# Weight sums of the MLP made once and kept in DRAM, in a trunk kernel whose order comes from the scheduler's detailed simulation

## The chip, the cores and the metric

The kernel runs on one core of one Trainium2 chip. The metric is the device time in microseconds of one execution; the median of three runs is compared, and the profile is of one more execution.

## The reference

One decoder layer over 2048 tokens of width 1024, in float32, with 256 memory tokens beside them:

```python
h = rmsnorm(x, mix_norm_g);  q, k, v, g, u = split(h @ w_in)
x = x + concat([silu(g) * head_rmsnorm(retention(rope(q), rope(k), v)), pool_mixer(u)]) @ w_out
x = x + cross_attn(rmsnorm(x, xa_norm_g), mem_n, xa_wq, xa_wkv, xa_wo)
a = rmsnorm(x, ffn_norm_g) @ w_up                  # 1024 -> 2 * 2816
c = conv_w[0] * a[t-2] + conv_w[1] * a[t-1] + conv_w[2] * a[t] + conv_b
x = x + (silu(c[gate half]) * c[value half]) @ w_down    # 2816 -> 1024
out = rmsnorm(x, final_norm_g)
```

## The kernel before

Tokens go in two batches of 1024 (`NB` = 2, `T` = 1024), each in two halves of 512 (`SUB`). Activations lie with channels on the 128 partitions. A product in full precision is made of three passes in float32r (`passes`, lines 227 to 229): each operand is split into a rounded high part, written by ScalarE, and the rest, written by VectorE or GpSimd.

**First stages, for each batch.** `unit` (line 271) makes one 128-wide output tile: `load_tile` (line 286) has SyncE's queue fetch 512 KB of weights into a raw buffer in tile `R`, `pairs` splits it into tile `Q` (lines 219 and 202), and 48 matmuls follow. Retention, pooling, the output projection, cross-attention and its projection are made of such units. Between them small matmuls of retention run, which `behind` hands out in steps: line 716 makes the scores of a head from its rotated q and k, and the last step of a rotation is an add on GpSimd (`tt(pool, d, d, w)` in `rope_evac`, tiles `Z<-Z,T`). During the first batch the stages fold weights as well (`folded_weights`, loads on line 403). Raw buffers: `R` holds five of 1024 columns.

**The MLP** is run by `run`. Both products use a scheme of seven products in place of eight: the weights of two output tiles and two halves of the inner dimension are blocks a11, a12, a21, a22, and the right side has two halves of channels and of tokens. A `Member` is one such pair of output tiles: `Up` (22 a batch) and `Down` (4 a batch in each of three rounds of inner tiles, with 3, 4 and 4 tiles a half). It has seven items, and each item needs one combination of the weight blocks and one of the right side:

- *Weights.* `fetch` loads four blocks of 256 KB (192 KB in the rounds of 3), and `add` makes a11 - a21, then a21 + a22, then that less a11, then a12 less that: four adds on GpSimd, tiles `R<-R`, line 202. `high` and `low` (lines 989 and 202) split the item's combination into a pair buffer. The tuple `how` says for each of the seven items who makes the low part: `""` VectorE, `"copy"` VectorE from a PSUM copy that ScalarE makes first (line 894), `"pool"` GpSimd.
- *Right side.* `combining` makes the tile in `G` for item i: it loads one or two pieces (`T<-Hd` or `T<-Gd`), subtracts on GpSimd if there are two (`T<-T`), and splits them (line 928 and 202). The tiles of the next round replace those of the last one as its last members are done with them, so they are made in the time of a few items at every change of round.
- *PE* runs an item as 12 matmuls (9 in the rounds of 3) into a PSUM bank. `evac` adds the banks up on VectorE; for `Up` the convolution, SiLU and the gate follow (lines 1064 to 1084), and the result goes to DRAM (`Gd`).

`run` writes the program in the order of the items with fetches, sums and splits some items ahead. At the end of each batch's last round the sums of squares are reduced by tiny matmuls (line 296) for the final norm, followed by two matmuls a half that spread the factors (line 1218).

What is written is not yet the order on the engines: the Tile framework's scheduler simulates the program, and puts on each engine next what is ready in that simulation. Each engine, and SyncE's queue of DMAs, then goes through its list strictly in order.

Of the kernel before, what the change touches and what calls it, by code (L numbers as in the profile page):

```python
# [29 lines left out]
TW = 576  # L30
EDGE = 16

_PI = 314159265358979323846264338327950288419716939937510582097494459
# [84 lines left out]
def trunk(ctx, tc, xT, memT, pos, w_qkgu, w_v, wkv, wqT, wo, wout_r, wout_p, poolT, w_up, w_dn, vecs, consts, outT):  # L118
# [82 lines left out]
    def tt(eng, out, a, b, op):  # L201
        return eng.tensor_tensor(out=out, in0=a, in1=b, op=op)  # L202
# [59 lines left out]

    behind = [iter(())]

# [4 lines left out]
    def unit(raw, rhs, evac, order=range(4)):  # L269


        hs = pairs(raw)
        ps = [mmps() for _ in range(NS)]
        for h in range(2):
            for s in range(NS):
                for j, kk in enumerate(order):
                    k = 4 * h + kk
                    w = [hs[h][:, i, kk * P : (kk + 1) * P] for i in range(2)]
                    passes(ps[s], w, rhs(k, s), h + j == 0, h == 1 and j == 3)
                next(behind[0], None)  # L280
                if h == 1:
                    evac(s, ps[s])
# [517 lines left out]
    def attention(sums, beside):  # L800
# [37 lines left out]
        for i in range(2 * KT):  # L838
# [20 lines left out]
            if late is not None:  # L859
                turn(*late)  # L860
            late = prob[hp], t, e
            next(more_m if i < KT - 2 else beside, None)

# [3 lines left out]
        return prob, end()  # L867

# [76 lines left out]
    class Member:  # L945


        def __init__(self, loads, halves):
            self.loads, self.n = loads, halves

            self.sign, self.how = 1, ("", "copy", "copy", "", "copy", "copy", "")
            self.raw = {}

        def fetch(self):

            g, h = ((0, 0), (1, 0), (1, 1), (0, 1))[len(self.raw)]
            w = self.n * P
            r = raws.take()
            sp.dma_start(r.f[:, :w], self.loads[g][:, h * w : (h + 1) * w])
            self.raw[g, h] = r  # L960

        def add(self, i):

            while len(self.raw) < (1, 2, 3, 3, 3, 4, 4)[i]:
                fetches.pop(0).fetch()
            w = self.n * P
            q = {k: r.f[:, :w] for k, r in self.raw.items()}
            a11, a12, a21, a22 = (q.get(k) for k in ((0, 0), (0, 1), (1, 0), (1, 1)))
            self.t = None
            if i == 1:  # L970
                self.t = H.take()
                x = self.t.f[:, :w]
                tt(pool, x, *((a11, a21) if self.sign > 0 else (a21, a11)), ALU.subtract)
            elif i == 2:

                tt(pool, a21, a21, a22, ALU.add)
                tt(pool, a11, a21, a11, ALU.subtract)
                x = a11
            elif i == 5:
                tt(pool, a11, a12, a11, ALU.subtract)  # L980
                x = a11
            else:
                x = {0: a11, 3: a22, 4: a21, 6: a12}[i]
            return x, self.t

        def high(self, i, x, pr):
            w = self.n * P
            p2 = pr.r.rearrange("p (i n) -> p i n", i=2)
            act.activation(p2[:, 0, :w], x, AF.Copy)  # L989
            return p2[:, 0, :w], p2[:, 1, :w]  # L990

        def low(self, i, x, t, hi, lo):
            low(x, hi, lo, self.how[i])
            if t is not None:
                t.free()
            if i >= 3:
                self.raw[{3: (1, 1), 4: (1, 0), 5: (0, 0), 6: (0, 1)}[i]].free()

# [3 lines left out]
    class Up(Member):  # L1002


        def __init__(self, b, f):
            super().__init__([w_up[f + g * NF].rearrange("p k n -> p (k n)") for g in range(2)], 4)
            self.b, self.f, self.how = b, f, ("", "copy", "copy", "", "copy", "copy", "pool")
            self.c = {}
# [81 lines left out]
    class Down(Member):  # L1090
# [3 lines left out]
        def __init__(self, b, j, at, k0, halves):  # L1094
            super().__init__([w_dn[2 * j + g][:, k0 : k0 + 2 * halves].rearrange("p k c -> p (k c)") for g in range(2)], halves)
            self.b, self.j, self.at, self.sign = b, j, at, -1

# [163 lines left out]
    def rounds():  # L1261
        out = []
        for b in range(NB):
            ups = [Up(b, f) for f in range(NF)]
            groups = [ups[:2]] + [[u] for u in ups[2:-2]] + [ups[-2:]]
            out.append(Round(lambda k, s, b=b: Hd[b, k][:, s * SUB : (s + 1) * SUB], range(4), range(4, 8), groups))
        for b in range(NB):
            for at, (k0, n) in enumerate(((0, 3), (6, 4), (14, 4))):
                ms = [Down(b, j, at, k0, n) for j in range(KT // 2)]
                out.append(Round(lambda k, s, b=b: Gd[b, k][:, s * SUB : (s + 1) * SUB], range(k0, k0 + n), range(k0 + n, k0 + 2 * n), [ms[:2], ms[2:]]))  # L1270
        out[1].shared = out[2].shared = True
        return out

    def run(rds):
        items = [(rd, g, m, i) for rd in rds for g in rd.groups for i in range(7) for m in g]
        fetches[:] = [m for rd in rds for g in rd.groups for _ in range(4) for m in g]
        made, added, highs = [], [], []

# [17 lines left out]
        def lows():  # L1296
            while highs:
                m, i, x, t, hi, lo = highs.pop(0)
                m.low(i, x, t, hi, lo)

        def fill():

            lows()
            if added and prs.room():
                m, i, x, t = added.pop(0)
                made.append(prs.take())
                highs.append((m, i, x, t, *m.high(i, x, made[-1])))
            k = len(made) + len(added)
            if k < len(items) and not added:
                m, i = items[k][2:]  # L1310
                added.append((m, i, *m.add(i)))
            while fetches and raws.room():
                fetches.pop(0).fetch()

# [80 lines left out]
    normed = norm_tables(room[:1])  # L1395
    wv.append(value_weights(3, Z.take()))
    for b in range(NB):

# [49 lines left out]
        for _ in beside:  # L1448
            pass
        Z = new_z(F32)  # L1450
        xs = [TT.take() for _ in range(NS)]
# [28 lines left out]
        for r in prob:  # L1480
            r.free()

        if b + 1 == NB:
# [163 lines left out]
```

## Time and profile before

| | us |
|---|---|
| median of three runs | 2580.94 (2580.14 to 2583.87) |
| the profiled execution | 2577.88 |
| its span, first to last instruction | 2576.1 |
| first stages, both batches | about 0 to 1198 |
| MLP, first to last product | about 1198 to 2551 |

A page of a profile gives the busy time of each engine, the span in 40 slices, and the costliest groups of instructions. In a table by stage each row is a stretch of the span, with busy us and number of instructions of each engine, the clock that TensorE was granted, the busy share of the DMA engines, and what they moved in GB/s. A row of a timeline is: start, duration, engine, line, operation, tiles written and read, and in square brackets how long the engine had been idle and what released it.

### The profile page before, as it was taken

Reading aid. Unit: us, or ns where it says so; the run is one execution under the profiler, and the core shown is the slowest. Engines: PE = TensorE matmul, PEld = TensorE weight load, DVE = VectorE, ACT = ScalarE, POOL = GpSimd, SP = SyncE. Lnnn points to the kernel's source line nnn. Section 1 sums busy time; section 2 is a strip of 40 time slices with the busy share of each in tenths; the row PEclk is TensorE's granted clock in tenths of the full one; section 3 lists DMA queues with packets and bytes.
Section 4 is the critical chain, followed back from the end, with each engine's and each line's share of the span. In section 5 each row is a group of like instructions: output and inputs, shape, how many; then the busy total and the mean of one; then the engine's idle time right before and its main releaser. Section 6 shows DMA issues by size and latency. Waiting matters only on the chain. (4 is left out here: it accounts for less than half of the span.)

```text
span 2576.1 us, 32736 instructions
## 1 busy us (share of the span) xinstructions
PE 2468.0 (96%) x11382; PEld 2045.6 (79%) x11382; DVE 1861.0 (72%) x2840; ACT 1246.6 (48%) x2240; POOL 816.4 (32%) x642
## 2 busy tenths in 40 slices
PE   7999999999999999998999999899999988989896
PEld 7888888888788888876788888688888866777675
DVE  8655564746736655435998888888888788888997
ACT  7334323534222234335555566555656574565654
POOL 0011130000301100014444445844444654543661
PEclk9999999999999999998999999899999999999998
DMA  8134424324311143144342223422222355548751
GB/s 289 49 101 141 132 83 150 115 90 141 137 33 41 35 142 119 40 169 155 106 160 98 86 94 131 147 82 86 84 89 90 136 179 184 188 165 266 252 168 70
DMA packets 166165, 323.74 MB, mean 126 GB/s; under 512 B 16752, under 2 KB 38896, under 8 KB 166000
## 3 DMA queue, kind: packets, MB, share of 16 engines
q1 hardware_dynamic: 140912, 292.29, 33.3%
q10 hardware_dynamic: 25088, 29.37, 3.3%
q8 instruction: 90, 1.47, 0.2%
q14 instruction: 75, 0.61, 0.1%
HBM read 249.76 MB, written 71.83 MB: 125 GB/s over the span
## 5 line engine op out<-in xcount | busy, mean ns | idle before, releaser
L227 PE MATMUL mm<-G,Q 128*128 128x512 f32 (+1 forms) x1944 | 755.8, 389 | 18.0 <-ACT Q L219 10.2
L228 PE MATMUL mm<-G,Q 128*128 128x512 f32 (+1 forms) x1944 | 750.1, 386 | 7.9 <-DVE G L202 7.9
L229 PE MATMUL mm<-G,Q 128*128 128x512 f32 (+1 forms) x1944 | 750.4, 386 | 7.0 <-DVE Q L202 6.9
L202 POOL TENSOR_TENSOR R<-R 128x512 f32<-128x512 f32 (+1 forms) x272 | 414.3, 1525 | 481.9 <-DMA R<-w_up 177.8
L227 PE MATMUL mm<-G 128*128 128x512 f32 (+1 forms) x1384 | 537.6, 389 | 20.4 <-DVE T L202 7.5
L228 PE MATMUL mm<-G 128*128 128x512 f32 (+1 forms) x1384 | 538.6, 389 | 16.4 <-DVE G L202 16.4
L229 PE MATMUL mm<-G 128*128 128x512 f32 (+1 forms) x1384 | 536.8, 388 | 0.0
L227 PEld LDWEIGHTS mm<-G,Q 128*128 128x128 f32 x1944 | 369.9, 190 | 91.3 <-ACT Q L219 10.6
L229 PEld LDWEIGHTS mm<-G,Q 128*128 128x128 f32 x1944 | 369.4, 190 | 82.2 <-DVE Q L202 9.6
L228 PEld LDWEIGHTS mm<-G,Q 128*128 128x128 f32 x1944 | 370.2, 190 | 80.0 <-DVE G L202 9.9
L227 PEld LDWEIGHTS mm<-G 128*128 128x128 f32 x1384 | 263.3, 190 | 77.6 <-DVE T L202 7.9
L228 PEld LDWEIGHTS mm<-G 128*128 128x128 f32 x1384 | 263.0, 190 | 75.0 <-DVE G L202 23.0
L229 PEld LDWEIGHTS mm<-G 128*128 128x128 f32 x1384 | 263.1, 190 | 52.1
L211 DVE SCALAR_TENSOR_TENSOR Z<-Z,vecs 128x1024 f32<-128x1024 f32 x176 | 254.0, 1443 | 69.8 <-ACT Z L1064 69.0
L202 DVE TENSOR_TENSOR Q<-R,Q 128x512 fp32r<-128x512 f32 (+1 forms) x234 | 175.8, 753 | 172.4 <-ACT Q L219 148.7
L202 POOL TENSOR_TENSOR T<-T 128x512 f32<-128x512 f32 (+3 forms) x140 | 203.7, 1465 | 279.3 <-PE mm L229 181.0
L202 DVE TENSOR_TENSOR Z<-Z,mm 128x512 f32<-128x512 f32 (+1 forms) x272 | 213.7, 786 | 28.7 <-PE mm L229 23.8
L894 ACT ACTIVATE aux<-R 128x512 f32<-128x512 f32 (+1 forms) x272 | 153.0, 580 | 152.6 <-POOL R L202 116.7
L202 POOL TENSOR_TENSOR Z<-Z,T 128x512 f32<-128x512 f32 x37 | 57.5, 1558 | 485.6 <-DVE T L202 398.1
L219 ACT ACTIVATE Q<-R 128x512 fp32r<-128x512 f32 x150 | 93.9, 628 | 237.1 <-PE mm L228 212.2
L928 ACT ACTIVATE G<-T 128x512 fp32r<-128x512 f32 x210 | 129.3, 628 | 155.7 <-POOL T L202 118.2
L202 DVE TENSOR_TENSOR G<-T,G 128x512 fp32r<-128x512 f32 (+1 forms) x211 | 173.2, 830 | 38.9 <-ACT G L219 18.7
(163 smaller groups left out, 2846.1 us busy)
## 6 DMA issues: line engine op xcount, KB each, us to landing
T<-Gd SPq DMA_DIRECT2D x198, 256.0 KB, 3.3
R<-w_up SPq DMA_DIRECT2D x176, 256.0 KB, 2.8
Gd<-Z SPq DMA_DIRECT2D x44, 512.0 KB, 2.6
T<-Hd SPq DMA_DIRECT2D x72, 256.0 KB, 3.1
R<-w_qkgu SPq DMA_DIRECT2D x32, 512.0 KB, 3.5
R<-w_dn SPq DMA_DIRECT2D x64, 256.0 KB, 3.3
T<-xT SPq DMA_DIRECT2D x48, 256.0 KB, 3.0
T<-Xd SPq DMA_DIRECT2D x48, 256.0 KB, 3.4
```

The lines of the kernel that those rows point to most:

```text
L202: return eng.tensor_tensor(out=out, in0=a, in1=b, op=op)
L211: dve.scalar_tensor_tensor(out=out, in0=a, scalar=s, in1=b, op0=op0, op1=op1)
L219: act.activation(hi, src, AF.Copy)
L227: pe.matmul(ps, lh, rh, start=start, stop=False)
L228: pe.matmul(ps, lh, rl, start=False, stop=False)
L229: pe.matmul(ps, ll, rh, start=False, stop=stop)
L894: act.activation(t, x, AF.Copy)
L928: act.activation(hi, x, AF.Copy)
```

## The change

1. `weight_sums` makes the four sums of each of the 34 different members (22 of `Up`, 12 of `Down`) once, during the first stages, and stores them in DRAM (`Ud`, `Dd`). Before, both batches made them. It has four buffers of 512 columns in the part of `R` that two of the five raw buffers had; three are left for the units. It is written as a generator, advanced at each half of a unit and at each step of attention.
2. A `Member` now loads seven blocks, one for each item: three as they are in the weights, four from `Ud` or `Dd`. There are ten raw buffers in the MLP in place of eight and two.
3. The tuples `how` change: the lows of items 2 and 6 are made on GpSimd, and two PSUM copies of `Up` go.
4. The context is made with `schedule_with_timeline_sim=True`: the scheduler orders the whole program by its detailed simulation.

The lines of the diff that carry this (what only renames or passes arguments on is left out):

```diff
+ROUNDS = ((0, 3), (6, 4), (14, 4))
...
+    Ud = drp.tile([NF, 4, P, SUB], F32, tag="Ud", name="Ud")
+    Dd = drp.tile([len(ROUNDS), KT // 2, 4, P, SUB], F32, tag="Dd", name="Dd")
...
                 next(behind[0], None)
+                next(under[0], None)
...
+    def weight_sums(spare):
+        jobs = [((w_up[f], w_up[f + NF]), 0, 4, Ud[f], 1) for f in range(NF)]
+        for at, (k0, n) in enumerate(ROUNDS):
+            jobs += [((w_dn[2 * j], w_dn[2 * j + 1]), k0, n, Dd[at, j], -1) for j in range(KT // 2)]
+        for w, k0, n, to, sign in jobs:
+            q = [spare.take() for _ in range(4)]
+            a11, a12, a21, a22 = (r.f[:, : n * P] for r in q)
+            for i, a in enumerate((a11, a12, a21, a22)):
+                sp.dma_start(a, block(w, i // 2, i % 2, k0, n))
+            yield
+            yield
+            tt(pool, a22, a21, a22, ALU.add)
+            tt(pool, a21, *((a11, a21) if sign > 0 else (a21, a11)), ALU.subtract)
+            yield
+            tt(pool, a11, a22, a11, ALU.subtract)
+            tt(pool, a12, a12, a11, ALU.subtract)
+            yield
+            for i, a in enumerate((a21, a11, a22, a12)):
+                sp.dma_start(to[i][:, : n * P], a)
+            for r in q:
+                r.free()
+            yield
...
-    def add(self, i):
...
-                tt(pool, x, *((a11, a21) if self.sign > 0 else (a21, a11)), ALU.subtract)
...
-                tt(pool, a21, a21, a22, ALU.add)
-                tt(pool, a11, a21, a11, ALU.subtract)
...
-                tt(pool, a11, a12, a11, ALU.subtract)
...
+            self.loads = [part(0, 0), own[0], own[1], part(1, 1), own[2], own[3], part(0, 1)]
...
+        def fetch(self, i):
+            r = raws.take()
+            sp.dma_start(r.f[:, : self.n * P], self.loads[i])
+            self.raw[i] = r
...
-            self.b, self.f, self.how = b, f, ("", "copy", "copy", "", "copy", "copy", "pool")
+            self.b, self.f, self.how = b, f, ("", "copy", "pool", "", "copy", "", "pool")
...
+            self.b, self.j, self.at, self.how = b, j, at, ("copy", "copy", "pool", "copy", "copy", "", "pool")
...
+    raws = Places([(R, j * T) for j in range(3)], T)
+    under[0] = weight_sums(Places([(R, 3 * T + i * SUB) for i in range(4)], SUB))
...
-    raws = Places([(R, j * SUB) for j in range(8)], SUB)
-    H = Places([(R, 4 * T + i * SUB) for i in range(2)], SUB)
+    for _ in under[0]:
+        pass
+    raws = Places([(R, j * SUB) for j in range(10)], SUB)
...
-    with tile.TileContext(nc) as tc:
+    with tile.TileContext(nc, schedule_with_timeline_sim=True) as tc:
```

What this does to the order, at three places. **GpSimd, the first rotations.** Here `R<-R` are the sums, `Z_70<-Z_70,T` the adds that end a rotation (four for each head: two halves of q, two of k). Before:

```order
L202 TENSOR_TENSOR Z_70<-Z_70 128x512
L202 TENSOR_TENSOR Z_70<-Z_70 128x256
L202 TENSOR_TENSOR T<-T,Z_70 128x256
L202 TENSOR_TENSOR Z_70<-Z_70,T 128x512 x16
L608 COPY T<-phalo 128x16
```

Now:

```order
L206 TENSOR_TENSOR T<-T,Z_70 128x256
L206 TENSOR_TENSOR R<-R 128x512 x35
L206 TENSOR_TENSOR Z_70<-Z_70,T 128x512
L206 TENSOR_TENSOR R<-R 128x512
L206 TENSOR_TENSOR Z_70<-Z_70,T 128x512
L206 TENSOR_TENSOR R<-R 128x512 x5
L206 TENSOR_TENSOR Z_70<-Z_70,T 128x512
L206 TENSOR_TENSOR R<-R 128x512
L206 TENSOR_TENSOR Z_70<-Z_70,T 128x512
L206 TENSOR_TENSOR R<-R 128x512 x14
L206 TENSOR_TENSOR Z_70<-Z_70,T 128x512
```

The scheduler has put 35 sums ahead of the first rotation's add, and it spreads the rest between them, 105 ahead of the first add for k of the last head; all 136 stand ahead of attention, not spread over both batches. SyncE's queue has the loads and stores of these sums between the units' loads in the same way.

**PE, the end of the first batch's last round.** `aux` on line 296 (now 301) are the sums of squares; the `mm` banks next to them are items of the second batch's first round, nine matmuls each. Before, the first two items of that round (18 matmuls) stand ahead of the sums:

```order
L227 MATMUL mm1177_17178<-G_69,Q_73 128x512
L228 MATMUL mm1177_17178<-G_69,Q_73 128x512
L229 MATMUL mm1177_17178<-G_69,Q_73 128x512
L296 MATMUL aux1178_17191<-consts_75,T_71 128x1 x8
L227 MATMUL mm1183_17226<-G_69,Q_73 128x512
L228 MATMUL mm1183_17226<-G_69,Q_73 128x512
```

Now six items and two thirds of the seventh (60 matmuls) do:

```order
L231 MATMUL mm1106_17504<-G_69 128x512
L232 MATMUL mm1106_17504<-G_69 128x512
L233 MATMUL mm1106_17504<-G_69 128x512
L301 MATMUL aux1092_17375<-consts_75,T_71 128x1 x8
L231 MATMUL mm1106_17504<-G_69 128x512
L232 MATMUL mm1106_17504<-G_69 128x512
```

The sums of squares moved 42 matmuls back.

**GpSimd, the start of the MLP.** `T<-T` belong to the right side, `R<-R` are weight sums, `G<-R,G` lows of weights. Before:

```order
L202 TENSOR_TENSOR T<-T 128x512 x4
L202 TENSOR_TENSOR R<-R 128x512
L202 TENSOR_TENSOR T<-T 128x512
L202 TENSOR_TENSOR R<-R 128x512 x2
L202 TENSOR_TENSOR T<-T 128x512 x2
L202 TENSOR_TENSOR R<-R 128x512
L202 TENSOR_TENSOR T<-T 128x512 x2
L202 TENSOR_TENSOR R<-R 128x512
L202 TENSOR_TENSOR T<-T 128x512
```

Now:

```order
L206 TENSOR_TENSOR T<-T 128x512
L1553 MEMSET Z_8489 128x2
L206 TENSOR_TENSOR T<-T 128x512 x6
L206 TENSOR_TENSOR G<-R,G 128x512 x2
L206 TENSOR_TENSOR T<-T 128x512 x7
L206 TENSOR_TENSOR G<-R,G 128x512 x2
```

The sums that stood between the subtractions of the right side are gone, and only lows of weights stand there.

More of the change, by code (lines that the diff above doesn't have):

```diff
@@ L261, in xpair @@
         return X[:, 2 * k, s * SUB : (s + 1) * SUB], X[:, 2 * k + 1, s * SUB : (s + 1) * SUB]
-    behind = [iter(())]
+    behind, under = [iter(())], [iter(())]
     def finish():
@@ L861, in attention @@
             late = prob[hp], t, e
+            next(under[0], None)
             next(more_m if i < KT - 2 else beside, None)
@@ L945, in trunk, with __init__ @@
     class Member:
-        def __init__(self, loads, halves):
-            self.loads, self.n = loads, halves
-            self.sign, self.how = 1, ("", "copy", "copy", "", "copy", "copy", "")
+        def __init__(self, w, sums, k0, halves):
+            self.n = halves
+            part = lambda g, h: block(w, g, h, k0, halves)
+            own = [sums[i][:, : halves * P] for i in range(4)]
+            self.loads = [part(0, 0), own[0], own[1], part(1, 1), own[2], own[3], part(0, 1)]
             self.raw = {}
-        def fetch(self):
-            g, h = ((0, 0), (1, 0), (1, 1), (0, 1))[len(self.raw)]
-            w = self.n * P
+        def fetch(self, i):
@@ L1275, in run @@
         items = [(rd, g, m, i) for rd in rds for g in rd.groups for i in range(7) for m in g]
-        fetches[:] = [m for rd in rds for g in rd.groups for _ in range(4) for m in g]
-        made, added, highs = [], [], []
+        fetches[:] = [(m, i) for _, _, m, i in items]
+        made, highs = [], []
         tiles, due, live = [], [], []
@@ L1297, in lows, with fetch @@
             while highs:
-                m, i, x, t, hi, lo = highs.pop(0)
-                m.low(i, x, t, hi, lo)
+                m, i, hi, lo = highs.pop(0)
+                m.low(i, hi, lo)
+        def fetch():
+            m, i = fetches.pop(0)
+            m.fetch(i)
         def fill():
             lows()
-            if added and prs.room():
-                m, i, x, t = added.pop(0)
+            if len(made) < len(items) and prs.room():
+                m, i = items[len(made)][2:]
+                while i not in m.raw:
+                    fetch()
                 made.append(prs.take())
[L1307 to L1311, printed above, removed]
+                highs.append((m, i, *m.high(i, made[-1])))
             while fetches and raws.room():
-                fetches.pop(0).fetch()
+                fetch()
         def advance():
@@ L1449, in trunk @@
             pass
+        under, paused = [iter(())], under
         Z = new_z(F32)
@@ L1481, in trunk @@
             r.free()
+        under = paused
         if b + 1 == NB:
```

40 lines of the change are left out of this document (10 added, 30 removed).

## The prediction

> **What bounds the kernel now.** I read the page first, then the table by stage, then what ended TensorE's idle time in the stages that lose. In the page's first part the numbers are busy us and share of the span:
>
> ```profile
> span 2576.1 us, 32736 instructions
> PE 2468.0 (96%) x11382; PEld 2045.6 (79%) x11382; DVE 1861.0 (72%) x2840; ACT 1246.6 (48%) x2240; POOL 816.4 (32%) x642
> ```
>
> PE is busy nearly throughout, and the change leaves it every matmul. Only time in which PE stands or runs at a lowered clock can be won, and the table says where that is:
>
> ```profile
> core 0: us, PE busy (x) PEld busy (x) DVE busy (x) ACT busy (x) POOL busy (x), PEclk, DMA share, GB/s
> 0.00:55.00 55.00, 40.94 (x303) 38.83 (x304) 47.20 (x86) 40.31 (x64) 6.29 (x9) 0.99 0.83 298
> 55.00:390.00 335.00, 333.56 (x1762) 286.70 (x1762) 204.63 (x415) 125.54 (x264) 45.46 (x42) 1.00 0.34 107
> ...
> 1180.00:1198.00 18.00, 13.70 (x46) 9.85 (x45) 12.97 (x16) 9.48 (x17) 9.72 (x7) 0.81 0.56 200
> 1198.00:1300.00 102.00, 91.52 (x397) 74.51 (x396) 83.43 (x108) 55.99 (x90) 48.99 (x36) 0.95 0.36 122
> 1300.00:1630.00 330.00, 330.00 (x1458) 273.34 (x1457) 280.25 (x324) 193.13 (x303) 168.63 (x132) 1.00 0.33 114
> 1630.00:1680.00 50.00, 40.22 (x147) 30.81 (x146) 43.88 (x46) 30.89 (x52) 39.76 (x29) 0.86 0.41 137
> 1680.00:2060.00 380.00, 380.00 (x1678) 314.67 (x1677) 310.59 (x363) 225.42 (x352) 182.42 (x152) 1.00 0.27 96
> 2060.00:2110.00 50.00, 41.66 (x162) 32.50 (x161) 42.49 (x58) 32.57 (x63) 27.66 (x20) 0.90 0.52 174
> 2110.00:2190.00 80.00, 73.10 (x300) 57.65 (x299) 66.79 (x89) 46.81 (x87) 41.85 (x30) 0.96 0.56 187
> 2190.00:2250.00 60.00, 55.65 (x237) 45.05 (x236) 53.31 (x66) 34.64 (x63) 37.02 (x26) 0.97 0.56 189
> ...
> 2300.00:2330.00 30.00, 20.11 (x82) 16.72 (x82) 25.81 (x46) 20.08 (x37) 11.21 (x9) 0.77 0.53 183
> 2330.00:2440.00 110.00, 99.19 (x416) 78.25 (x415) 101.88 (x141) 65.58 (x126) 56.52 (x40) 0.97 0.77 257
> 2440.00:2551.00 111.00, 108.21 (x475) 88.45 (x473) 100.47 (x131) 63.12 (x111) 44.93 (x31) 1.00 0.35 116
> 2551.00:2576.10 25.10, 4.92 (x22) 3.04 (x20) 13.33 (x32) 3.63 (x6) 6.19 (x5) 0.59 0.45 167
> ```
>
> Where PE never stands (1680 to 2060) a matmul takes 380/1678 = 0.2265 us. A stage's loss is its length less its matmuls times that, clock included. 1180 to 1198 loses 7.6 us, then 12.1, 16.7 (1630 to 1680, the change from the first batch of `Up` to the second), 13.3, 12.1, 6.3, 11.4, 15.8 and 3.4: 99 us in all. The two long stretches of `Up` lose nothing, so all that the change takes from the other engines there is worth nothing by itself. The start (14 us) and the tail (20 us) it hardly touches.
>
> **The MLP's part.** The sums go from GpSimd, lows come to it:
>
> ```profile
> L202 POOL TENSOR_TENSOR R<-R 128x512 f32<-128x512 f32 (+1 forms) x272 | 414.3, 1525 | 481.9 <-DMA R<-w_up 177.8 <-DVE Q L202 89.3 <-DMA R<-w_dn 88.3
> L202 POOL TENSOR_TENSOR G<-R,G 128x512 fp32r<-128x512 f32 x44 | 63.6, 1447 | 8.9 <-ACT G L989 7.7 <-PE aux L1218 1.2
> L202 DVE TENSOR_TENSOR Q<-R,Q 128x512 fp32r<-128x512 f32 (+1 forms) x234 | 175.8, 753 | 172.4 <-ACT Q L219 148.7 <-ACT Q L989 23.2
> L894 ACT ACTIVATE aux<-R 128x512 f32<-128x512 f32 (+1 forms) x272 | 153.0, 580 | 152.6 <-POOL R L202 116.7 <-DVE Q L202 23.1 <-DVE G L202 9.8
> ```
>
> GpSimd loses 272 adds of 1.525 us (414 us) and gets 44 + 2 x 24 = 92 lows of 1.447 us (133 us). VectorE loses those 92 lows, about 0.75 us each: 69 us. ScalarE loses 88 copies of 0.58 us: 51 us. What these are worth is read where PE loses.
>
> (a) *Start of the MLP, 19.7 us lost.* The longest gap, engine by engine in order of time:
>
> ```profile
> 1207.77 1.26 POOL L202 TENSOR_TENSOR R<-R 128x512 f32<-128x512 f32 x1 [4.06 <-DMA R<-w_up]
> 1208.98 1.26 POOL L202 TENSOR_TENSOR T<-T 128x512 f32<-128x512 f32 x1
> 1210.28 1.15 ACT L928 ACTIVATE G<-T 128x512 fp32r<-128x512 f32 x2 [2.54 <-POOL T L202]
> 1210.94 1.29 DVE L202 TENSOR_TENSOR G<-T,G 128x512 fp32r<-128x512 f32 x1 [2.92 <-ACT G L928]
> 1215.29 0.79 PE L227 MATMUL mm<-G 128*128 128x512 f32 x1 [7.51 <-DVE T L202]
> ```
>
> GpSimd waits 4.06 us for a weight block, adds for 1.26, and only then makes the right side's subtraction that PE waits for. Without the sum that subtraction is up to 5.3 us earlier; next to be late are the other tiles' own loads. With the clock that a shorter gap keeps I take 9 of the 19.7.
>
> (b) *Change to the second batch, 16.7 us lost.* GpSimd is busy 39.76 of 50 us with the right side's subtractions and lows and with sums between them. A member of `Up` is 7 items of 12 matmuls, 84 x 0.2265 = 19 us, so 50 us hold 2.6 members, so about 10 sums of 1.525 go and 2.6 lows of 1.447 come: 12 us less in a chain that lacks 16.7. Loads and VectorE (43.88 of 50) stay in it: I take 8.
>
> (c) *The rounds of `Down` but for the sums of squares, 51 us lost in five stages.* VectorE is busy 101.88 of 110 us in the worst. At 63 or 84 matmuls a member 110 us hold about 6, so 12 of its lows go, 9 us, and 24 sums against 12 lows leave GpSimd 19 us freer. Against it, three more loads of 192 or 256 KB a member, about 4.5 MB in 110 us, 40 GB/s on top of 257 at a DMA share of 0.77. I take half: 25.
>
> (d) *Sums of squares, 11.4 us lost.* PE stands for them with its next items ready behind:
>
> ```profile
> 2319.63 0.59 PE L296 MATMUL aux<-consts,T 128*128 128x1 f32 x2 [9.89 <-DVE T L202]
> ```
>
> The new order puts 42 matmuls more ahead of them, 42 x 0.2265 = 9.5 us of work into a gap of 9.89. I take 10, since the clock (0.77 in that stage) is kept too.
>
> Together 52 us of 99. Three more loads for each of 68 members (52 MB over 1350 us, 38 GB/s) cost nothing in `Up`, at 96 to 114 GB/s: a load lands in about 3 us, and ten buffers reach ten items, 27 us, ahead. Without that cover each would be 3 us on PE.
>
> **The first stages' part.** 136 sums of at most 1.525 us go on a GpSimd that is busy 45.46 of 335 us: 207 us fit. But their chain is serial, four buffers hold one member, and SyncE's list has the units' loads behind stores that wait for GpSimd, GpSimd's has the rotations' adds behind sums that wait for loads. The whole chain must therefore keep the pace at which the order threads it:
>
> ```profile
> 53.45 0.43 SPq L403 DMA_DIRECT2D R<-wqT  x1
> 161.42 1.05 PE L716 MATMUL aux<-Z 128*128 128x128 f32 x8
> 324.74 0.72 PE L716 MATMUL aux<-Z 128*128 128x128 f32 x5
> ```
>
> The first four sums' loads stand about there (53 us). The scores of the first head run at 161.4 and need a k whose add has 41 sums ahead, 10.25 members: (161.4 - 1.3 - 54)/10.25 = 10.3 us a member. Those of the last head (324.7, in the new order 18 matmuls earlier: 320.7) have 105 ahead, 26.25 members: 10.1 us. I count nothing for the units' loads, which lie some steps ahead of their matmuls. The pace comes from these:
>
> ```profile
> L202 POOL TENSOR_TENSOR R<-R x272: 993/1305/2285, 1146.9 to 2517.6; 128x512 f32<-128x512 f32 x120, 128x384 f32<-128x384 f32 x16
> Hd<-T SPq DMA_DIRECT2D x32, 256.0 KB, 2.4
> R<-w_up SPq DMA_DIRECT2D x176, 256.0 KB, 2.8
> R<-w_dn SPq DMA_DIRECT2D x19, 256.0 KB, 4.2
> ```
>
> A buffer goes through two adds, a store, and the next member's load before its next add. Low: 2 x 1.305 + 2.4 + 2.8 + 0.2 for issue = 8.0 us. High, with both transfers as they land in the 257 GB/s stage (the 4.2 us row is from 2330 to 2440): 2 x 1.525 + 2 x 4.2 + 0.2 = 11.7 us. A member moves 2.1 MB, 200 GB/s at 10.5 us, on top of 107: nearer to the busy row, but with four transfers at a time, not dozens. I take 10.5. Lateness at the last head: 0.4 x 26.25 = 10.5 us, of which nothing comes back, since PE takes its list in order; with 3 us of lowered clock and 2 us for the first member's loads and its store's wait ahead of others on SyncE at the start, 15. Bounds: 0 (nothing here shortens anything) and 1.6 x 26.25 + 8 = 50.
>
> The Trainium skill's page "DMA: Bandwidth & Descriptors" (Anatomy of one DMA) fits a transfer by 2.0 us plus its bytes at 436 GB/s, 2.6 us for 256 KB; by it a member would take about 8.5 us, and this part cost 2 instead of 15. The 4.2 us row says that it doesn't hold in a busy stage.
>
> VectorE and GpSimd hinder each other: the adds of the row above take 1.305 us at the median and up to 2.285. The Trainium skill's page "SBUF — State Buffer" (two separate sides) calls it an exclusive lock between GpSimd and VectorE's operations with two SBUF inputs, whoever comes second waiting out the other's whole instruction; by it an add could wait out one such operation (0.75 us), a member 1.5, and 10.5 would be 12.0, an estimate that leans to rival 3; the spread of the adds agrees, how often they meet in the first stages no trace here shows.
>
> Two raw buffers fewer cost nothing: three units of 48 matmuls (10.9 us each) cover a landing of 3 to 4 us.
>
> **Sum.** 2577.9 (the profiled execution) - 52 + 15 = 2541; that execution was 3 us under the median of the runs, 2580.9, so 2544 for a median.
>
> **The rivals.**
> 1. *The chain of sums keeps pace and the right side was held by GpSimd alone*: cost 2, gain 75 of 99: 2508. For it: GpSimd's 80% in (b), the wait in (a). Against it: VectorE's 93% in the worst stage.
> 2. *The changes of round are not GpSimd's*: loads and VectorE end them, only (d) and a part of (a) come, 17, and the early part costs 15: 2579. For it: 257 GB/s there already, with 40 more to come.
> 3. *The chain of sums sets the pace of the first stages*, slower: rotations' adds wait on GpSimd behind sums that wait for DMAs, and PE waits at each head. At 12.5 us a member it is 2.4 x 26.25 = 63 us and some 12 of lowered clock; with the gain of 52, 2604. It decides from 52/26.25 + 10.1 = 12.1 us a member, clock apart. For it: the 11.7 above; against: PE's delay thins out the other transfers, which frees DMAs.
>
> **How the numbers follow.** Forecast 0.47, rival 1 0.20, rival 2 0.18, rival 3 0.15. The forecast alone spans 2521 (early cost 2, gain 62) to 2574 (35 and 42). The range reaches through half of rival 1 and through rival 2 with an early cost 13 higher: 2508 to 2592; outside are about 0.10 below and 0.10 above. A measurement of this kernel tells about 0.2%, 5 us. Faster by more: forecast 0.46, rival 1 0.20, rival 2 0.08, 0.74. Within: 0.01 + 0.06, 0.07. Slower: rival 3 0.15, rival 2 0.04, 0.19.
>
> **What would show it.** Right: PE's loss between 2300 and 2330 all but gone; GpSimd under 55% at the change of batches; 34 members' sums done by about 410 us, PE's waits in the first 400 us at the first small matmuls of each head, 10 us in sum. Wrong: no wait there (rival 1), or over 50 us of it, with GpSimd waiting for `R<-w_up` and SyncE for GpSimd (rival 3); or stages of `Down` that still lose 40 us with VectorE and loads as releasers (rival 2).

## The result and the profile after

The changed kernel takes 2597.28 us, median of four runs (2594.76 to 2599.5), against 2582.09 (2580.14 to 2583.87) before: ratio 1.0062, 95% interval 1.0048 to 1.0076. It is 15 us slower, where 37 us faster was forecast. The profiled execution took 2599.5 us. Its page begins:

```profile
span 2597.7 us, 33544 instructions
PE 2475.1 (95%) x11382; PEld 2053.3 (79%) x11382; DVE 1878.0 (72%) x2748; ACT 1200.0 (46%) x2150; POOL 728.4 (28%) x598
```

VectorE has 92 instructions fewer than before and is busy 17 us longer. That is the first hint. The table by stage of the changed kernel:

```profile
core 0: us, PE busy (x) PEld busy (x) DVE busy (x) ACT busy (x) POOL busy (x), PEclk, DMA share, GB/s
0.00:62.00 62.00, 41.09 (x260) 38.88 (x261) 52.50 (x87) 40.38 (x62) 8.99 (x10) 0.92 0.81 292
62.00:190.00 128.00, 120.11 (x624) 102.47 (x624) 89.61 (x110) 41.77 (x76) 70.21 (x47) 0.96 0.69 231
190.00:460.00 270.00, 237.91 (x1174) 199.38 (x1173) 186.18 (x297) 77.74 (x186) 155.38 (x127) 0.94 0.77 254
460.00:705.00 245.00, 244.36 (x1111) 201.73 (x1111) 143.08 (x274) 101.71 (x202) 5.82 (x4) 1.00 0.41 141
...
1220.00:1330.00 110.00, 100.95 (x439) 82.55 (x438) 78.50 (x111) 57.34 (x94) 31.38 (x25) 0.97 0.53 168
...
1690.00:1725.00 35.00, 28.97 (x116) 22.00 (x115) 35.00 (x32) 21.65 (x37) 26.69 (x18) 0.95 0.54 174
```

The loss lies where the sums are made, up to some 470 us; right after, PE is full again. A fair measure across kernels is when PE reaches its k-th large matmul, since all of them run the same 10,464. The 4,900th stands just ahead of the MLP (1178.9 us before). There the changed kernel is 68.7 us behind; from there to the last it wins 48.3 back. Both numbers for every kernel that follows, in us against the kernel before (minus is ahead; worked out from the traces), with the median of the runs. Each trace is one execution, and the executions of one kernel differ by 2 to 15 us, so that a few us between two rows say nothing by themselves:

```
                                                 at 4,900th  from there on   median
after          the changed kernel                   +68.7       -48.3        2597.28
sched_only     before + detailed simulation          +4.2       -33.6        2551.13
no_detail      after - detailed simulation         +122.0       -27.5        2670.29
no_sums        after, sums not made                  +2.3       -50.6        2533.25
paced          after, sums' loads held back         +34.6       -50.9        2561.70
dma_only       after, sums' transfers alone         +30.5       -51.0        2558.41
loads_only     after, sums' loads alone             +19.7       -47.3        2550.22
dma_paced      transfers alone, held back            +3.0       -50.2        2531.28
adds_only      after, sums' adds alone              +56.6       -46.0        2584.72
adds_dve       adds alone, on VectorE               +23.4       -46.9        2552.26
rot_dve        after, rotations' adds on VectorE    +54.0       -46.2        2583.42
paced_rot      paced, rotations' adds on VectorE    +29.4       -52.3        2555.10
sums_dve       after, sums' adds on VectorE         +57.7       -48.6        2580.24
dve_own        the same, DMAs issued by GpSimd      +48.8       -45.8        2575.05
paced_dve      paced, sums' adds on VectorE                                  2549.95
paced_dve1     the same, one add to a step          +22.5       -48.0        2550.79
```

One execution of `paced_dve` fell to a clock of 0.75 (3084 us), and it was the profiled one, so its trace is not used.

Who waits in the first stages of the changed kernel (columns: engine, line and tile that wait, what for, us in total, times, longest):

```profile
POOL R L206 <- DMA R<-w_up: 98.4, 29, 11.3
POOL R L206 <- DMA R<-w_dn: 40.0, 14, 8.7
ACT Q L223 <- DMA R<-w_qkgu: 32.2, 5, 9.8
ACT G L223 <- DMA R<-wqT: 22.0, 3, 13.8
PE aux L721 <- POOL Z L206: 11.5, 3, 6.9
```

and in SyncE's queue, over the same time:

```profile
SPq L899 <- POOL R L206: 117.6, 96, 4.7
SPq L889 <- DMA Ud<-R: 60.8, 42, 4.4
```

GpSimd waits 138 us for the sums' loads; SyncE 118 us for GpSimd before it can store, and 61 us for stores before the next member's loads; behind SyncE ScalarE waits 54 us for weights of the units. These are rival 3's signs. But PE's own wait for GpSimd (line 721, a head's scores) is 11.5 us, not over 50.

### The profile page after: what moved, and what is told of

Its sections match the earlier page's. It is cut to its first block, busy times and chain, and to the rows that moved or that the text cites. A ratio compares the mean times of both kernels' runs of the same rounds, so it can differ in the third digit from the quotient of the medians.

```text
span 2597.7 us, 33544 instructions
## 1 busy us (share of the span) xinstructions
PE 2475.1 (95%) x11382; PEld 2053.3 (79%) x11382; DVE 1878.0 (72%) x2748; ACT 1200.0 (46%) x2150; POOL 728.4 (28%) x598
## 4 chain that ended last, share of the span: by engine, by line
PE 69%; DMA 10%; DVE 9%; POOL 5%; issue 4%; ACT 2%; SPq 1%; DVEq 0%; POOLq 0%; ACTq 0%
PE mm L231 22%; PE mm L232 22%; PE mm L233 22%; DVE G L206 3%; DMA R<-w_up 3%; POOL R L206 3%; DVE Z L206 2%; DVE T L206 2%; DMA T<-Gd 2%; DMA Ud<-R 1%; DMA T<-Hd 1%; POOL T L206 1%; DMA R<-w_dn 1%; DVE Q L206 1%; POOL G L206 1%
## 5 line engine op out<-in xcount | busy, mean ns | idle before, releaser
L215 DVE SCALAR_TENSOR_TENSOR Z<-Z,vecs 128x1024 f32<-128x1024 f32 x176 | 239.8, 1365 | 45.5 <-ACT Z L1070 44.2
L206 POOL TENSOR_TENSOR R<-R 128x512 f32<-128x512 f32 (+1 forms) x136 | 192.6, 1416 | 212.0 <-DMA R<-w_up 128.1
L206 POOL TENSOR_TENSOR G<-R,G 128x512 fp32r<-128x512 f32 (+1 forms) x100 | 149.5, 1497 | 350.2 <-ACT G L998 316.7
L206 DVE TENSOR_TENSOR Q<-R,Q 128x512 fp32r<-128x512 f32 x198 | 153.7, 778 | 124.7 <-ACT Q L223 118.9
L998 ACT ACTIVATE G<-R 128x512 fp32r<-128x512 f32 (+1 forms) x272 | 163.7, 612 | 172.1 <-PE mm L232 157.7
L206 DVE TENSOR_TENSOR G<-T,G 128x512 fp32r<-128x512 f32 (+1 forms) x211 | 180.5, 870 | 35.5 <-ACT G L962 19.3
L206 DVE TENSOR_TENSOR G<-R,G 128x512 fp32r<-128x512 f32 (+1 forms) x169 | 149.5, 897 | 56.4 <-ACT G L223 50.0
```

Of the source, the lines that this page charges most:

```text
L215: dve.scalar_tensor_tensor(out=out, in0=a, scalar=s, in1=b, op0=op0, op1=op1)
L998: act.activation(p2[:, 0, :w], self.raw[i].f[:, :w], AF.Copy)
```

## The experiments

A theory on record before the first runs was A, the chain of sums threaded tightly through lists that are taken in order; its rivals were B, the detailed simulation's own order, and C, the missing raw buffers. Later expectations count 168 adds of sums and 63 or 110 MB. There are 136 adds (34 members), and 136 blocks (120 of 256 KB, 16 of 192) loaded and stored once are 69 MB.

### Which part of the change

**The detailed simulation alone.** The kernel before, with one edit:

```diff
-    with tile.TileContext(nc) as tc:
+    with tile.TileContext(nc, schedule_with_timeline_sim=True) as tc:
```

> The kernel before, with the detailed simulation as the only change. Theory A (the first stages' 72 us come from the chain of sums, which sits tightly threaded in lists that are followed in order): there is no chain here, so the first stages stay as before, and the sums of squares move back: 2565 to 2575. Theory B (the detailed simulation's order itself costs the first stages their time): 2620 or more, with PE's waits at the heads' small matmuls. Theory C (three raw buffers for the units in place of five): 2565 to 2575, five buffers here.

2551.13, ratio 0.9876 (0.9860 to 0.9893): faster than any theory had it. B falls: by the MLP only 4.2 us are lost. From there on 33.6 us are won with no sum moved, where the changed kernel wins 48.3.

**All but the detailed simulation.** The same line the other way, in the changed kernel:

> The changed kernel without the detailed simulation. Its list for GpSimd has 33 sums ahead of the first rotation's add and 115 ahead of the last head's, about as many as the changed kernel's. Theory A: the first stages lose 60 to 80 us all the same, the MLP's part wins some 40 (the sums of squares not among it): 2600 to 2615. Theory B: the first stages lose nothing, 2535 to 2550. Theory C: as theory A, 2600 to 2615.

2670.29, ratio 1.0334 (1.0318 to 1.0349), far above the expectation: in the scheduler's usual order the rest of the change costs the first stages 122 us, with the detailed order 68.7. Whether C has a part in the 68.7, the next run says; for the 122 no run does.

**No sums made.** The members load plain blocks in their place, with three raw buffers and the detailed order:

```diff
-            own = [sums[i][:, : halves * P] for i in range(4)]
+            own = [part(1, 0), part(0, 1), part(1, 0), part(0, 1)]
...
-    under[0] = weight_sums(Places([(R, 3 * T + i * SUB) for i in range(4)], SUB))
```

> The changed kernel without the making of the sums: items 1, 2, 4 and 5 of each member load a plain weight block in place of a sum, so the transfers in the MLP are the same and the output is not the reference's. Three raw buffers and the detailed simulation stay. Theory A: the first stages are as before, the MLP as in the changed kernel: 2520 to 2535. Theories B and C: the first stages lose 60 to 75 us as in the changed kernel, about 2595.

2533.25, ratio 0.9804 (0.9790 to 0.9819). B and C are out: all three raws and the detailed order are here, and PE reaches the MLP 2.3 us late. The sums cost 68.7 - 2.3 = 66 us. The run also bounds the idea: were the sums free, the kernel would be 18 us ahead of the detailed simulation alone (2551).

**The sums' loads held back.** `anchor` is the latest load of a unit's weights; a member's loads are placed behind it, and a member takes six steps in place of five:

```diff
-            for i, a in enumerate((a11, a12, a21, a22)):
-                sp.dma_start(a, block(w, i // 2, i % 2, k0, n))
+            with tc.issue_after(anchor[0].ins):
+                for i, a in enumerate((a11, a12, a21, a22)):
+                    sp.dma_start(a, block(w, i // 2, i % 2, k0, n))
+            yield
```

> The changed kernel with the sums spread out: the four loads of a member stand on SyncE behind the newest load of the units, attention or projection at that place of the program, and a member takes six steps in place of five, so the 34 members go over both batches (8 sums ahead of the first rotation's add, 40 ahead of the last head's, 64 by the first attention). Theory A: the chain is far slower than it could be and nobody waits for it, 2525 to 2545, faster than both kernels. Theories B and C: about 2590, as neither the order's making nor the raw buffers change. If the sums' transfers and adds cost by their amount, not by their place in the lists, about 2590 too.

2561.7, ratio 0.9918 (0.9903 to 0.9933). The chain's last add now ends at 989 us in place of 474, and half of the 66 us goes; 32 stay, where theory A expected none.

### Adds or transfers

**Transfers alone.** The four `tt(pool, ...)` lines of `weight_sums` are taken out:

> The changed kernel without the four adds of each member: the sums' loads and stores stay, the sums stored are wrong, so the output is not the reference's. The sums cost the first stages 66 us (the 1,200 first us against the kernel that makes none). If that cost is GpSimd's list (list theory: a rotation's add stands behind 55 adds that wait for loads), most of it goes: about 2545 to 2555, with PE's waits for GpSimd's Z gone. If it is SyncE's list (a store that waits for GpSimd, with the units' loads behind it), the stores now wait for their loads alone and about half stays: 2560 to 2580. If it is the 63 MB moved beside the units' own loads (transfer theory), all of it stays: 2590 to 2600.

**Adds alone.** Loads and stores are taken out, and members load plain blocks as in `no_sums`; the adds take whatever the buffers hold:

> The changed kernel without the sums' loads and stores: the four adds of each member stay, on whatever the buffers hold, and the rounds load plain blocks, so the output is not the reference's. By the list theory nothing is left for the adds to wait for, and their own 6.3 us of GpSimd a member lie in its idle time: about 2535 to 2548, near the 2533 of the kernel without sums. If GpSimd's busy time itself is the cost (168 adds of 1.5 us ahead of and among the rotations' adds), 2560 to 2590.

Transfers alone: 2558.41, 28 us lost against `no_sums`, between what the record gave for GpSimd's list and for SyncE's. Adds alone: 2584.72, 54 us lost, with not one load for them to wait for. The list theory gave 2535 to 2548; it is wrong about the larger part. Nor is it GpSimd's busy time ahead of the rotations' adds, the other theory, though the time lies in its range: 55 adds stand ahead of the first rotation's, and yet from 60 to 460 us all waits of other engines for GpSimd come to 2.8 us. VectorE's groups show what it is. From 62 to 460 us without sums (after the bar: busy us, mean ns of one):

```profile
L206 DVE TENSOR_TENSOR Q<-R,Q 128x512 fp32r<-128x512 f32 x53 | 36.9, 697 | 52.5 <-ACT Q L223 52.2
L206 DVE TENSOR_TENSOR G<-R,G 128x512 fp32r<-128x512 f32 x41 | 29.8, 754 | 31.6 <-ACT G L223 31.5
L206 DVE TENSOR_TENSOR T<-mm,Z 64x512 f32<-64x512 f32 x32 | 22.0, 688 | 0.6
L215 DVE SCALAR_TENSOR_TENSOR T<-T 128x512 f32<-128x512 f32 x17 | 11.4, 688 | 0.3
L212 DVE TENSOR_SCALAR T<-T 128x512 f32<-128x512 f32 x6 | 2.5, 422 | 0.1
```

and with the adds alone, in the same stretch (the last row is GpSimd's):

```profile
L206 DVE TENSOR_TENSOR G<-R,G 128x512 fp32r<-128x512 f32 x41 | 45.5, 1145 | 25.0 <-ACT G L223 25.0
L206 DVE TENSOR_TENSOR Q<-R,Q 128x512 fp32r<-128x512 f32 x43 | 38.8, 903 | 25.8 <-ACT Q L223 25.6
L215 DVE SCALAR_TENSOR_TENSOR T<-T 128x512 f32<-128x512 f32 x17 | 24.6, 1464 | 0.3
L206 DVE TENSOR_TENSOR T<-mm,Z 64x512 f32<-64x512 f32 x32 | 22.0, 689 | 0.6
L212 DVE TENSOR_SCALAR T<-T 128x512 f32<-128x512 f32 x6 | 8.4, 1394 | 0.1
L206 POOL TENSOR_TENSOR R<-R 128x512 f32<-128x512 f32 (+1 forms) x134 | 192.5, 1447 | 34.2 <-DVE Q L206 27.2
```

The same VectorE instructions take 1.3 to 3.3 times as long in the mean, but for those with an input in PSUM (`mm`): 688 and 689 ns. In the timeline of GpSimd, then of VectorE, in this run:

```profile
93.64 32.41 POOL L206 TENSOR_TENSOR R<-R 128x512 f32<-128x512 f32 x20
```

```profile
106.69 6.86 DVE L215 SCALAR_TENSOR_TENSOR T<-T 128x512 f32<-128x512 f32 x4
```

While GpSimd makes 20 adds in a row, one each 32.41/20 = 1.62 us, VectorE makes four of its own in 6.86, 1.71 us each instead of 0.69: one for one, in step. They take turns. The changed kernel shows the same, in the same stretch:

```profile
L206 DVE TENSOR_TENSOR G<-R,G 128x512 fp32r<-128x512 f32 x41 | 41.7, 1051 | 47.7 <-ACT G L223 45.9 <-PE mm L233 1.6 <-DMA Ud<-R 0.2
L206 DVE TENSOR_TENSOR Q<-R,Q 128x512 fp32r<-128x512 f32 x40 | 40.2, 1006 | 38.6 <-ACT Q L223 38.3
L206 POOL TENSOR_TENSOR R<-R 128x512 f32<-128x512 f32 (+1 forms) x131 | 183.7, 1402 | 170.1 <-DMA R<-w_up 98.4 <-DMA R<-w_dn 40.0 <-issue 26.0
```

`Q<-R,Q` and `G<-R,G` are low parts of weights (in `G`, of those that are folded), which PE's next matmuls need. How this reaches PE is seen at its longest gap with the adds alone. Four lows take 6.70 us beside GpSimd's adds; only as they are done can SyncE refill the raw buffers, so ScalarE waits 16.13 us for the next folded weights, and PE 9.94 us for a split that stands behind these on ScalarE:

```profile
151.32 6.70 DVE L206 TENSOR_TENSOR G<-R,G 128x512 fp32r<-128x512 f32 x4
158.44 1.15 ACT L223 ACTIVATE G<-R 128x512 fp32r<-128x512 f32 x2 [16.13 <-DMA R<-wqT]
163.84 0.79 PE L231 MATMUL mm<-G,Q 128*128 128x512 f32 x1 [9.94 <-ACT Q L223]
```

The Trainium skill's page "SBUF — State Buffer" (Who interferes with whom) says it so: a GpSimd instruction that reads SBUF and a VectorE one with two SBUF inputs shut each other out, and so do GpSimd and a VectorE instruction in a mode that uses both ports; the second to issue waits out the whole first one. The trace agrees for two inputs, with the numbers above; no row says which mode the slowed one-input instructions ran in.

**The adds alone, on VectorE**, in place of GpSimd, is the test of that:

```diff
-            tt(pool, a22, a21, a22, ALU.add)
+            tt(dve, a22, a21, a22, ALU.add)
```

(and so the other three).

> The run with the adds alone (no loads or stores of the sums, plain blocks in the rounds, so the output is not the reference's), its 168 adds now on VectorE. On GpSimd they took 1.49 us each and cost 51 us of the whole, while VectorE's instructions with both inputs in SBUF went from 0.69 to 1.18 to 1.52 us wherever they lay beside one. Lock theory (the two engines take turns at SBUF, so each add of GpSimd costs VectorE about 1 us): the same adds at 0.69 us on VectorE are 116 us of it and hold nobody, 2540 to 2555. If the cost is instead that an add, on whatever engine, stands ahead of what PE waits for in a list: 2580 or later, since VectorE's list serves more waiting products than GpSimd's.

2552.26, within the lock theory's range; the other theory had it at 2580 or later. From 62 to 460 us:

```profile
L206 DVE TENSOR_TENSOR R<-R 128x512 f32<-128x512 f32 (+1 forms) x134 | 95.5, 733 | 0.8
L206 DVE TENSOR_TENSOR Q<-R,Q 128x512 fp32r<-128x512 f32 x49 | 34.1, 696 | 29.4 <-ACT Q L223 29.1
L206 DVE TENSOR_TENSOR G<-R,G 128x512 fp32r<-128x512 f32 x41 | 28.4, 713 | 19.5 <-ACT G L223 16.7 <-PE mm L233 2.7
```

Giving VectorE 96 us more work makes the kernel 32 us faster, since its other instructions are back at 0.70 us. That the two engines lock each other out is shown, and it is what the adds cost beyond VectorE's own time, since in neither run the others wait for GpSimd's list by more than a few us. 21 us against `no_sums` stay.

### The transfers' part

> The run with the sums' transfers alone, without the stores too (168 loads of 256 KB stay, plain blocks in the rounds, so the output is not the reference's). If the cost is the stores that wait for their loads' landing in SyncE's list, with a unit's loads behind them, most of the 28 us goes: 2533 to 2542. If it is that the sums' loads take the engines that a unit's loads need, about half stays, as half of the bytes do: 2543 to 2552.

> The run with the sums' transfers alone (no adds, so the output is not the reference's; 2558, 28 us behind the kernel without sums by 1,180 us), with each member's loads placed behind the latest load of a unit in the order and one step more a member. If those 28 us come from where the transfers stand in SyncE's list and when they meet a unit's loads, most goes: 2533 to 2542. If the 110 MB moved cost the same wherever they lie: 2550 to 2560.

`loads_only` is `dma_only` without the stores and with plain blocks in the rounds; `dma_paced` is `paced` without its adds. Without stores 2550.22, 17 us lost, all of it by the 1,000th matmul (229 us): no store holds the loads now, and the last is issued at 212 us. Held back, 2531.28: all 69 MB, 0.7 us lost. From 62 to 460 us, the transfers alone, then held back:

```profile
62.00:190.00 128.00, 121.44 (x658) 104.93 (x657) 63.58 (x116) 42.77 (x77) 5.66 (x4) 0.99 0.89 294
190.00:460.00 270.00, 257.62 (x1305) 217.40 (x1304) 161.35 (x323) 92.07 (x209) 36.93 (x38) 0.99 0.78 257
```

```profile
62.00:190.00 128.00, 128.00 (x700) 111.47 (x700) 68.96 (x131) 46.25 (x88) 6.19 (x4) 1.00 0.40 131
190.00:460.00 270.00, 270.00 (x1365) 229.22 (x1364) 170.33 (x326) 99.02 (x213) 38.46 (x38) 1.00 0.66 216
```

At 294 GB/s PE loses; at 131 and 216 it loses nothing. A unit's load of 512 KB (median us to landing) in `no_sums`, then in `dma_only`, then in `dma_paced`:

```profile
R<-w_qkgu SPq DMA_DIRECT2D x14, 512.0 KB, 3.8
```

```profile
R<-w_qkgu SPq DMA_DIRECT2D x15, 512.0 KB, 6.0
```

```profile
R<-w_qkgu SPq DMA_DIRECT2D x15, 512.0 KB, 4.0
```

So the transfers cost by when they come, not by how many they are. Place and pace were changed together; which of them does it isn't separated. `paced` has the same transfers and the adds besides, and is 34.6 - 3.0 = 32 us later at the MLP: what holding back leaves of the sums' cost is the adds'.

### The lists, and versions that are better

**The rotations' adds on VectorE** takes away what the prediction had PE wait for:

```diff
-                tt(pool, d, d, w, ALU.add)
+                tt(dve, d, d, w, ALU.add)
```

> The changed kernel with the add of the rotation on VectorE in place of GpSimd: nobody's product waits for GpSimd's list in the first stages then, only the sums' own stores do. If GpSimd's list is what costs most, 2550 to 2570. If it is SyncE's list (loads behind stores that wait), the gaps of PE move from small matmuls that wait for Z to large ones that wait for folded weights, and the time stays at 2585 to 2600.

> The paced kernel (2562; sums' loads behind the unit's loads in the order, one step more a member) with the add of the rotation on VectorE. It still lost some 32 us to the sums in the first stages, part of it at small matmuls that wait for GpSimd's Z and part at folded weights. List theory: the first part goes, 2545 to 2555. If VectorE, 85 of every 100 us busy at times in these stages, pays for the added adds: 2560 to 2575.

2583.42 and 2555.10: 14 and 7 us better (the intervals of `paced` and `paced_rot` overlap, so the 7 are not sure). So the rotation's add behind the sums was worth some 14 of the 66 us, and GpSimd's list isn't what costs most. `rot_dve` comes out just under what SyncE's list was given, `paced_rot` at the upper edge of the list theory.

**The sums' adds on VectorE** in the full kernels:

> The changed kernel with the four adds of each member on VectorE. Lock theory alone: about 2560, the time of the run with the sums' transfers alone and a little of VectorE's. List theory: an add that waits for its loads now stops VectorE's list, ahead of folded weights and masks, and the waits of 138 us that GpSimd spent for these loads fall on VectorE: 2620 or later.

> The changed kernel with the sums' adds on VectorE and the sums' loads and stores issued by GpSimd in place of SyncE. If the cost of the transfers (25 us in the run with transfers alone) is SyncE's list, where a unit's loads stand behind a store that waits, it goes: 2540 to 2560. If it is the traffic itself, or if VectorE's list stops for loads, 2570 to 2620. Against the same kernel with SyncE's issues the difference is the list's alone.

> The paced kernel (2562; sums' loads behind a unit's own loads in the order) with the adds on VectorE. Lock theory: the loads stand well ahead of the adds, so VectorE seldom waits and pays 0.69 us an add: 2540 to 2552. List theory: 2560 to 2590, as VectorE stops for loads.

`sums_dve` at 2580.24 lies between its two forecasts and shows both effects at once: no lock, but 54.5 us in which VectorE stands for `R<-w_up`, 16.8 for `R<-w_dn`. With GpSimd's queue issuing the sums' DMAs (`dve_own`) 2575.05, 5 us less, so SyncE's list looks like a small part; whether issuing from GpSimd has a price of its own no run shows. Held back as well (`paced_dve`), 2549.95, within the lock theory's range.

**One add to a step** (six steps as in `paced_dve`, the stores behind the fourth add; the first add comes two steps after its loads, there three):

> The paced kernel with the sums' adds on VectorE, one add to a step instead of two (still six steps a member, the stores behind the fourth add). The transfers paced alone cost nothing (2531), so the 17 us that the paced kernel with adds on VectorE still loses (2550) are its 168 adds. If they are pairs of adds that hold VectorE's list 1.4 us at a time, or a wait for loads: 2536 to 2545. If it is VectorE's time as such, some 100 us in stages where it is two thirds busy: 2546 to 2552.

2550.79 (ratio 0.9886, 0.9866 to 0.9906), the same as `paced_dve`, in the range that was given to VectorE's time as such. The sums on VectorE, over 62 to 1180 us:

```profile
L206 DVE TENSOR_TENSOR R<-R 128x512 f32<-128x512 f32 (+1 forms) x135 | 101.0, 748 | 59.0 <-DMA R<-w_up 33.8 <-DMA R<-w_dn 23.7
```

101 us of adds and 59 us of waiting for their loads, on the engine that makes PE's low parts. It beats both kernels, but equals the detailed simulation alone (2551.13): the 15 to 18 us that finished sums win the MLP are what making them costs. How the last 20 us split between VectorE's time and its waits stays open.

## Why the prediction was wrong

**The MLP's part (52) was right in size: 48.3.** By the 5,300th matmul the lead is 9.4 us ((a) said 9), by the 6,900th 8.0 more ((b) said 8), from there on 30.9 ((c) and (d): 35). In the change of batches 35 us hold 116 matmuls: 35 - 116 x 0.2265 = 8.7 us lost, where 16.7 were. But GpSimd is busy 26.69 of those 35 us, not under 55%, and VectorE all 35.00: VectorE, not GpSimd, is the one without idle time there now. In (a) the gap that was read as GpSimd's ends with VectorE in its own row (`<-DVE T`): an evacuation at 1214.56 us, behind five low parts in VectorE's list, of which the late subtraction held up the first. In (d) the wait for the sums of squares is gone, and the next is late:

```profile
2367.92 0.79 PE L1224 MATMUL aux<-Q,ones 128*128 128x512 f32 x1 [6.68 <-DVE Q L206]
```

The cause was in part credited wrongly. I gave 42 of the 52 to the sums and lows that leave GpSimd and VectorE, and 10 to the new order. But `sched_only` wins 33.6 with the old sums, and `no_detail` 27.5 with the old order; together they win 48.3, so the two overlap, and the moved work adds only 15 to 17 to the flag. Only the 8.0 us of (b) are plainly the moved work's: in that stretch `sched_only` wins nothing, and `no_detail` 6.1. That the total came out near 52 is therefore partly luck. Over the whole kernel part 4 of the change, one flag, is the part that pays.

**The start ("hardly touches").** The 200th matmul (37.5 us before) comes 13.9 us late, and 13.2 in `sched_only`: that is the detailed order (1.0 in `no_detail`), and some 9 of it are made up by the MLP.

**The first stages' part (15) is the step that failed: the sums alone cost 66.** Three of its terms:

1. *The chain.* Pace and start were both off. The changed kernel's sums on GpSimd begin:

```profile
46.28 3.06 POOL L206 TENSOR_TENSOR R<-R 128x512 f32<-128x512 f32 x1 [29.65 <-DMA R<-w_up]
75.39 4.70 POOL L206 TENSOR_TENSOR R<-R 128x512 f32<-128x512 f32 x3 [26.05 <-issue]
...
182.19 1.27 POOL L206 TENSOR_TENSOR Z<-Z,T 128x512 f32<-128x512 f32 x1
...
377.33 1.26 POOL L206 TENSOR_TENSOR Z<-Z,T 128x512 f32<-128x512 f32 x1
```

From 75.4, not 54, to the last head's add at 377.33: (377.33 - 75.39)/26.25 = 11.5 us a member, not 10.5. Put into the prediction's own formula these give 377.3 - 319.4 = 58 us late, close to what was lost, and yet the formula isn't the cause: with that add taken off GpSimd, `rot_dve` still loses 54.0 - 2.3 = 52. PE was late for other reasons, and the list with it. Rival 3 had the sign and nearly the time (2604), by a mechanism worth 14 us.

2. *The lock.* The prediction saw that the two engines hinder each other and priced it on GpSimd's adds, 1.5 us a member, though not in the 10.5 of its sum. It left out the other direction: VectorE, whose weight lows feed PE directly, waits as long for GpSimd. Same adds, other engine: 33 us (56.6 against 23.4). "207 us fit" on an idle GpSimd was true, and beside the point.

3. *"Nothing for the units' loads."* Transfers alone cost 28 us when they come at 257 to 294 GB/s, and 0.7 us when spread; I had priced the landing of the sums' loads and not that of the units' beside them. The fit that the prediction quotes from the Trainium skill's page "DMA: Bandwidth & Descriptors" (Anatomy of one DMA) is given there for DMAs that GpSimd issues, and the sums' loads are SyncE's: those of `w_up` land in 3.9 us at the median in the changed kernel, from 60 to 460 us, and not in 2.6.

The parts overlap (54 and 28 alone, 66 together): probably an engine made late by one hides some of the other; no run takes this apart. Of the 66, about 21 us are TensorE's clock: in the table 128 us at 0.96 and 270 at 0.94, where `no_sums` has 1.00 in both.

## What to carry to other kernels

Before moving work to an idle engine, ask what it shares with the busy one: time the busy engine's own instructions beside such work (here 0.69 us alone, 1.7 beside GpSimd's adds), not only the idle engine's gaps. Work that is made ahead of time isn't free because engines have time for it: here its transfers cost 28 us in a crowd and 0.7 us when spread behind the urgent loads, and its adds cost the first stages time on either engine, 20 us at best. When a change bundles a scheduling flag with a restructuring, run each alone: here the flag alone won 31 us, and the rest lost 46.

## What the runs showed of the hardware that was not expected

- VectorE beside GpSimd's adds: 0.69 us becomes 1.7 (two SBUF inputs), and an instruction with one SBUF input goes from 0.42 to 1.39; with an input in PSUM 0.69 stays.
- Short gaps cost clock too. In the changed kernel PE stands 2.56 us at 181 to 183.5 us for GpSimd's `Z`, and no longer gap lies in the 17 us that follow:

```profile
183.00:200.00 17.00, 16.49 (x89) 14.30 (x90) 10.78 (x13) 5.79 (x12) 10.12 (x8) 0.90 0.84 286
```

A mean of 0.90 over 17 us is 3.4 us at half clock. The Trainium skill's page "TensorE: Matmul & The Clock Gate" (HAM oscillation) tells kernels to have no gap over about 3.4 us; here one of 2.56 was enough. The length alone doesn't settle it: PE stands 3.12 us from 258.5 us on too, and the granted clock is 1.00 from 258 to 277 us.
- A load of 512 KB that lands in 3.8 us takes 6.0 beside a chain of loads and stores that moves 257 to 294 GB/s.
